# Two transformer-like blocks on one core: a seven-product matrix scheme rewritten without GpSimd, and four smaller moves of work

## The chip, the cores and the metric

One Trainium2 chip, one core. The metric is device time in microseconds (us) from one execution's start to its end; three runs of the kernel before gave 2943.02 to 2946.54, median 2946.03.

## The reference

512 tokens of width 1024, in float32, pass through one block of a first kind and two layers of a second kind.

```python
def first_block(x, ...):
    proj = rmsnorm(x, ln1_g) @ w_in               # q, k, v, pool, z, xbc, dt, gates
    y_a = dilated_attention_mixer(q, k, v, rel_bias) @ w_a
    y_b = pool_mixer(pool_in, pool_w, pool_scale) @ w_b
    y_c = ssd_mixer(z, xbc, dt_raw, ...) @ w_c    # state-space scan in chunks of 128
    x = x + (gates[0] * y_a + gates[1] * y_b + gates[2] * y_c) @ w_o
    x = x + conv_ffn(rmsnorm(x, ln2_g), ...)      # 2816 wide
    return rmsnorm(x, final_g)

def second_block(h, ...):                          # two layers
    proj = rms_norm(h, attn_norm[l]) @ w_in[l]
    a = differential attention; r = bidirectional retention; c = grouped-query attention
    h = h + (sum of gates[n] * (branch n @ w_branch[l, n])) @ w_out[l]
    h = h + square(relu(rms_norm(h, mlp_norm[l]) @ w_mlp_in[l])) @ w_mlp_out[l]   # 4096 wide
    return h
```

## The kernel before, in words

**Precision.** A float32 operand is split (`split`, L293) into a rounded high part, cast on ScalarE (L294), and a low part, subtracted on VectorE (L295). A product is then three matmuls: high by high, high by low, low by high. `feat` (L263) gives features by tokens, `tok` (L273) tokens by columns.

**Weights.** They come by SP's DMA queue into `raw` buffers of 128 x 1024 (`RAWS` of them, L25), and `halve` (L235) splits each into one `whi` and one `wlo` buffer (`HALVES` of each, L26). A block of 256 columns for all 1024 rows is two halves, a block of 512 columns is four (`wide`, L257).

**Pages.** Everything else lies in 47 pages of 128 x 512 (`Arena`, L50). PSUM has three `mm`, four `ax` and one `po` bank.

**Order.** The program is written in one order, with generators that are woven by step counts (`weave`, L178); a scheduler then fixes each engine's own order by when it expects operands to be ready, the program's order deciding between ready ones. At run time every engine works through its list in order.

**`quick` (L928)** multiplies a merged or hidden matrix of 512 tokens by a weight of at most 1024 rows and 1024 columns and adds the result to the residual pages X. It is Winograd's form of Strassen's scheme: both matrices are cut in 2 x 2 blocks, seven products in place of eight. It is called 14 times: for `w_o`, for three pieces of the feed-forward's second weight, and in each layer for `w_out` and four pieces of `w_mlp_out`. The token side is prepared by `Forms` (L68): each pair of finished pages r1, r2 (`add`, then `make`, L85) yields S1, S2, A11 - A21 and A12 - S2 by four operations on halves of pages, 128 x 256 (three on GpSimd, L89 to L91, one on VectorE, L92, which overwrites a half that L89 reads), and then the parts of all of them (`split`). The weight side takes four sums of weight blocks (`combine`, L948), each in two operations of 128 x 1024, of which the second is GpSimd's (L950). The seven products (`product`, L952) run in the order 1, 5, 3, 6, 2, 7, 4; products 1 and 5 leave out their last of four row blocks at first, since that is the pair of pages that gets ready last, and do it after both. Product 3 adds in PSUM to 5, and 4 to 7. Product 1, and later its sum with 6, is kept in two pages u, and `add_u` (L971, L973) adds these to X with eight GpSimd operations of 128 x 512. The other sums are `add` (L964) on VectorE.

**After some calls** come row norms. `rows` and `turn`, given to `quick`, make the norm of a row tile (`row_rstd`, L321, `norm_rows`, L333) and turn it by TensorE transposes into the next U (`norm_turn`, L341). `power` (L308) is GpSimd's x to the -1/2. At the end of the first block `rows` (L1127) does two norms at once, final and next, one power after the other.

**State-space scan** (`ssd`, L808): `start` (L838) multiplies a triangle of ones by high and low parts of the decays, 128 x 512 each, high on VectorE, low on GpSimd (L845).

**Grouped-query projection** (`gqa_proj`, L1520): keys and values, then queries, are projected, normed and rotated (GpSimd ends the rotation, L1227 and L1228), and `to_feat` turns them by transposes. In `layer` (L1637) it is chained between the rest of the first gate and three steps of the second (`take(gr, 3)`), woven with retention; grouped-query attention follows.

Of the kernel before, what the change touches and what calls it, by code (L numbers as in the profile page):

```python
# [10 lines left out]
F32 = mybir.dt.float32  # L11
F32R = mybir.dt.float32r
AF = mybir.ActivationFunctionType
# [11 lines left out]
RAWS = 5  # L25
HALVES = 6  # L26
# [44 lines left out]
class Forms:  # L71
# [13 lines left out]
    def make(self, r1, r2):  # L85
        B = self.body
        g, v, c, d = B.nc.gpsimd, B.nc.vector, slice(0, 256), slice(256, 512)
# [30 lines left out]
class Body:  # L118
# [189 lines left out]
    def power(self, out, x, n):  # L308
        self.nc.gpsimd.tensor_tensor(out, x, self.mhalf[:, :n], op=ALU.pow)

    def rstd(self, ss, n, eps):
        v, r = self.st(n), self.st(n)
        self.nc.vector.tensor_scalar(v, ss, eps, None, op0=ALU.add)
        self.power(r, v, n)
        return r
# [5 lines left out]
    def row_rstd(self, x, ss=None):  # L321

        nc = self.nc
        v, r = self.st(1), self.st(1)
# [315 lines left out]
    def gated(self, U, wg, g0, bias, y, wy, kt, acc, first, last, perm=False):  # L640
# [8 lines left out]
        for i in range(8 + AHEAD):  # L649
# [23 lines left out]
            t = T.pop(c)  # L673
            if first:
# [13 lines left out]
        self.free(y)  # L688
# [119 lines left out]
    def ssd(self, xs, BC, dt):  # L808
# [29 lines left out]
        def start(i):  # L838
# [4 lines left out]
            for q in range(2):  # L843
                for r, part, eng in zip(R[i][q], parts, (nc.vector, nc.gpsimd)):
                    eng.tensor_tensor(hl(r.t), self.tri.unsqueeze(1).to_broadcast([P, 4, P]),  # L845
                                      part[:, c, 8 * g + 4 * q:8 * g + 4 * q + 4].bitcast(F32).unsqueeze(2).to_broadcast([P, 4, P]), op=ALU.mult)
# [81 lines left out]
    def quick(self, w, k0, kt, F, X, scale=1.0, rows=None, turn=None):  # L928
# [8 lines left out]
        engines = (nc.vector, nc.gpsimd)  # L937
# [33 lines left out]
        def add_u(t, h, u):  # L971
            x = X[t][h].t
            nc.gpsimd.tensor_tensor(x, x, u.t, op=ALU.add)  # L973

# [15 lines left out]
        u = self.pgs(2)  # L990
# [15 lines left out]
        combine(b12, b22, b12, ALU.subtract)  # L1006
        b11 = [load(1, 1, j) for j in js]
        combine(b11, b12, b11, ALU.add)
        W6 = right(b11)
        for q in two:  # L1010
            add(q, 1, d[q])
        b = bank()
        product(6, W6, b)
        W7 = right(b12)
        b21 = [load(2, 1, j) for j in js]
        W2 = right(b21)
        for q in two:
            if scale == 1.0:
                nc.vector.tensor_tensor(u[q].t, u[q].t, b[q], op=ALU.add)
            else:  # L1020
                nc.vector.scalar_tensor_tensor(u[q].t, b[q], scale, u[q].t, op0=ALU.mult, op1=ALU.add)
            add_u(q, 1, u[q])
            sums(q)
        for q in two:
            add_u(2 + q, 1, u[q])
            add_u(2 + q, 0, u[q])
        e = bank()
        product(2, W2, e)
        combine(b21, b21, b11, ALU.subtract)
        for q in two:  # L1030
            add(q, 0, e[q])
# [746 lines left out]
```

## Time and profile before

| what | us |
|---|---|
| median of three runs | 2946.03 |
| the profiled execution | 2942.34 |
| its span, first to last instruction | 2940.2 |
| TensorE matmul busy | 2830.1 |
| VectorE busy | 2041.5 |
| ScalarE busy | 1307.2 |
| GpSimd busy | 938.3 |

The profile covers one execution. A matmul is listed from its start to a modelled end and overlaps the next, so a mean duration is longer than the distance between two starts. "Idle before" an instruction is put down to what released it last.

### The profile page before, as it was taken

What the parts mean: (1) busy time and instruction counts of PE and PEld (TensorE: products, weight loads), DVE (VectorE), ACT (ScalarE), POOL (GpSimd) and SP (SyncE); (2) the same over time, 40 slices, a digit from 0 to 9 for tenths busy, and PEclk for the clock granted to TensorE, in tenths of its full rate; (3) what the DMA queues carried; (4) which work ended last, traced back from release to release, by engine and by line L of the source; (5) the groups of instructions that cost most, each with busy time, mean ns of one, the idle gap of its engine ahead of it and who ended that gap; (6) DMA issues with size and microseconds to landing.
All of it is one profiled execution on the core that took longest, in us unless ns stands there. A gap on an engine that the chain in (4) does not pass through costs nothing.

```text
span 2940.2 us, 36920 instructions
## 1 busy us (share of the span) xinstructions
PE 2830.1 (96%) x13639; PEld 2361.2 (80%) x13639; DVE 2041.5 (69%) x3316; ACT 1307.2 (44%) x2249; POOL 938.3 (32%) x763
## 2 busy tenths in 40 slices
PE   8999999998999979999999899999999999989999
PEld 7888887887877868888787777787888887778777
DVE  4345477757778786856776787777765766877776
ACT  4344243334444445553464444444554455444443
POOL 0001105314132244211632344345321432534444
PEclk9999999999999989999999999999999999999999
DMA  7243331324242432222222332344222222323341
GB/s 217 82 126 105 100 97 55 88 77 151 74 142 72 133 112 87 88 75 73 73 69 68 118 112 88 101 130 149 84 65 89 64 67 61 122 83 115 115 129 65
DMA packets 225655, 288.20 MB, mean 98 GB/s; under 512 B 17769, under 2 KB 155331, under 8 KB 225475
## 3 DMA queue, kind: packets, MB, share of 16 engines
q1 hardware_dynamic: 212288, 272.77, 30.4%
q10 hardware_dynamic: 13187, 13.08, 1.5%
q8 instruction: 107, 1.75, 0.2%
q14 instruction: 73, 0.60, 0.1%
HBM read 276.30 MB, written 11.67 MB: 98 GB/s over the span
## 4 chain that ended last, share of the span: by engine, by line
PE 76%; DVE 8%; POOL 7%; DMA 4%; ACT 2%; issue 2%; ACTq 0%; SPq 0%; POOLq 0%; DVEq 0%
PE mm L270 14%; PE mm L269 14%; PE mm L271 14%; PE mm L280 4%; PE mm L281 4%; PE mm L282 4%; PE ax L960 4%; PE ax L961 4%; PE ax L962 4%; PE ax L301 3%; DVE wlo L295 3%; POOL raw L950 2%; DMA raw<-in_w_mlp_out_dram 2%; POOL pg L89 1%; DVE pg L295 1%
## 5 line engine op out<-in xcount | busy, mean ns | idle before, releaser
L295 DVE TENSOR_TENSOR wlo<-raw,whi 128x1024 fp32r<-128x1024 f32 (+3 forms) x554 | 730.3, 1325 | 276.6 <-ACT whi L294 269.1
L294 ACT CAST whi<-raw 128x1024 fp32r<-128x1024 f32 (+3 forms) x554 | 565.4, 1031 | 591.3 <-PE mm L270 318.0
L270 PE MATMUL mm<-ul,whi 128*128 128x512 f32 (+1 forms) x1792 | 689.2, 385 | 5.7 <-DVE ul L295 5.7
L269 PE MATMUL mm<-uh,whi 128*128 128x512 f32 (+1 forms) x1792 | 690.8, 387 | 2.0 <-ACT uh L294 2.0
L271 PE MATMUL mm<-uh,wlo 128*128 128x512 f32 (+1 forms) x1792 | 687.4, 384 | 0.0
L270 PEld LDWEIGHTS mm<-ul,whi 128*128 128x128 f32 x1792 | 340.7, 190 | 71.1 <-DVE ul L295 7.0
L269 PEld LDWEIGHTS mm<-uh,whi 128*128 128x128 f32 x1792 | 339.8, 190 | 66.8 <-ACT uh L294 2.9
L271 PEld LDWEIGHTS mm<-uh,wlo 128*128 128x128 f32 x1792 | 340.6, 190 | 64.7 <-issue 0.6
L960 PE MATMUL ax<-whi,pg 128*128 128x512 f32 x770 | 309.6, 406 | 55.2 <-ACT pg L294 43.8
L961 PE MATMUL ax<-wlo,pg 128*128 128x512 f32 x770 | 309.2, 402 | 0.0
L962 PE MATMUL ax<-whi,pg 128*128 128x512 f32 x770 | 298.0, 398 | 0.0
L280 PE MATMUL mm<-whi,uh 128*128 128x512 f32 (+3 forms) x736 | 280.5, 381 | 1.5 <-ACT uh L294 1.5
L281 PE MATMUL mm<-wlo,uh 128*128 128x512 f32 (+3 forms) x736 | 278.1, 378 | 0.0
L282 PE MATMUL mm<-whi,ul 128*128 128x512 f32 (+3 forms) x736 | 278.0, 378 | 0.0
L294 ACT CAST pg<-pg 128x512 fp32r<-128x512 f32 (+2 forms) x264 | 144.9, 574 | 261.8 <-DVE pg L92 66.3
L950 POOL TENSOR_TENSOR raw<-raw,raw 128x1024 f32<-128x1024 f32 (+1 forms) x56 | 159.2, 2843 | 314.7 <-DVE wlo L295 152.4
L973 POOL TENSOR_TENSOR pg<-pg,pg 128x512 f32<-128x512 f32 x112 | 209.6, 1895 | 91.0 <-ACT pg L998 48.5
L295 DVE TENSOR_TENSOR pg<-pg,pg 128x512 fp32r<-128x512 f32 (+2 forms) x264 | 198.1, 776 | 53.3 <-ACT pg L294 51.3
L960 PEld LDWEIGHTS ax<-whi,pg 128*128 128x128 f32 x770 | 149.3, 194 | 98.5 <-ACT pg L294 50.2
L89 POOL TENSOR_TENSOR pg<-pg,pg 128x256 f32<-128x256 f32 x55 | 59.1, 1075 | 421.5 <-DVE pg L1677 163.8
L301 PE MATMUL ax<-c_k_ident,pg 128*128 128x128 f32 x993 | 150.6, 279 | 33.4 <-DVE pg L1146 10.8
L962 PEld LDWEIGHTS ax<-whi,pg 128*128 128x128 f32 x770 | 149.4, 194 | 32.8 <-DVE pg L295 0.4
(264 smaller groups left out, 4387.1 us busy)
## 6 DMA issues: line engine op xcount, KB each, us to landing
raw<-in_w_in_dram SPq DMA_DIRECT2D x180, 512.0 KB, 3.7
raw<-in_w_mlp_out_dram SPq DMA_DIRECT2D x80, 512.0 KB, 3.6
raw<-in_w_mlp_in_dram SPq DMA_DIRECT2D x64, 512.0 KB, 4.3
raw<-in_ffn_w_up_dram SPq DMA_DIRECT2D x44, 512.0 KB, 3.8
raw<-in_ffn_w_down_dram SPq DMA_DIRECT2D x25, 512.0 KB, 3.5
raw<-in_w_out_dram SPq DMA_DIRECT2D x20, 512.0 KB, 3.7
raw<-in_w_branch_dram SPq DMA_DIRECT2D x16, 512.0 KB, 3.9
raw<-in_w_o_dram SPq DMA_DIRECT2D x10, 512.0 KB, 4.3
```

Source lines behind the costliest of these rows:

```text
L269: mm(ps, hi[:, cols], uh, start=k == 0, stop=False)
L270: mm(ps, hi[:, cols], ul, start=False, stop=False)
L271: mm(ps, lo[:, cols], uh, start=False, stop=k == nk - 1)
L280: mm(ps, uh, hi, start=k == 0, stop=False)
L281: mm(ps, uh, lo, start=False, stop=False)
L282: mm(ps, ul, hi, start=False, stop=k == n - 1)
L294: self.nc.scalar.copy(hi, src)
L295: self.nc.vector.tensor_tensor(lo, src, hi.bitcast(F32), op=ALU.subtract)
L301: self.nc.tensor.transpose(pt[:, i * P:(i + 1) * P], s, self.ident)
L960: mm(ps, uh[:, c], hi, start=not more and k == 0, stop=False, skip_group_check=more)
L961: mm(ps, uh[:, c], lo, start=False, stop=False, skip_group_check=more)
L962: mm(ps, ul[:, c], hi, start=False, stop=k == n - 1, skip_group_check=more)
```

## The change

`quick` is put in another order, 1, 2, 5, 6, 3, 7, 4, in which all of products 6, 7 and 4 add in PSUM to product 1, and product 2 has two `mm` banks of its own. The pages u and `add_u` are gone; all sums, those of weights and those of `Forms.make` too, are VectorE's. Each call loads as many weight blocks as before: the block B21 is read twice in place of B11. The other edits: 7 raw buffers and 5 half buffers; the low parts in `ssd.start` as four scaled ScalarE copies of 128 x 128 each; the gate steps in `gqa_proj` between the query projection and the turns; the two powers of `rows` from two means, r2 = (f + eps m + eps squared) to the -1/2, without the first power; and `free(y)` in `gated` at its last use.

```diff
-RAWS = 5
-HALVES = 6
+RAWS = 7
+HALVES = 5
...
-        g.tensor_tensor(s.t[:, c], r1.t[:, d], r2.t[:, d], op=ALU.add)
-        g.tensor_tensor(s.t[:, d], s.t[:, c], r1.t[:, c], op=ALU.subtract)
-        g.tensor_tensor(w.t[:, c], r2.t[:, c], s.t[:, d], op=ALU.subtract)
+        v.tensor_tensor(s.t[:, c], r1.t[:, d], r2.t[:, d], op=ALU.add)
         v.tensor_tensor(r1.t[:, d], r1.t[:, c], r1.t[:, d], op=ALU.subtract)
+        v.tensor_tensor(s.t[:, d], s.t[:, c], r1.t[:, c], op=ALU.subtract)
+        v.tensor_tensor(w.t[:, c], r2.t[:, c], s.t[:, d], op=ALU.subtract)
...
-        nc.vector.scalar_tensor_tensor(v, ss[:, 0:1], EPS, ss[:, 1:2], op0=ALU.add, op1=ALU.add)
-        self.power(r, v, 1)
-        return r
+        v = self.st(1)
+        nc.vector.tensor_tensor(v, ss[:, 0:1], ss[:, 1:2], op=ALU.add)
+        return self.rstd(v, 1, EPS)
...
+                hi, lo = [x[:, c, h0:h0 + 4].bitcast(F32) for x in parts]
+                for h in range(4):
+                    nc.scalar.activation(self.cols(R[i][q][1].t, h), self.tri, AF.Copy, scale=lo[:, h:h + 1])
...
         def combine(out, x, y, op):
-            for j, (o, a, b) in enumerate(zip(out, x, y)):
-                engines[j % 2].tensor_tensor(o, a, b, op=op)
+            for o, a, b in zip(out, x, y):
+                nc.vector.tensor_tensor(o, a, b, op=op)
...
         product(1, W1, a, b=n - 1)
-        u = self.pgs(2)
+        W2 = right([load(2, 1, j) for j in js])
+        e = [self.mm() for _ in two]
+        product(2, W2, e, b=n - 1)
+        product(1, W1, a, a=n - 1)
+        product(2, W2, e, a=n - 1)
         b12 = [load(1, 2, j) for j in js]
         combine(b11, b12, b11, ALU.subtract)
         W5 = right(b11)
         d = bank()
-        product(5, W5, d, b=n - 1)
-        product(1, W1, a, a=n - 1)
+        product(5, W5, d)
         for q in two:
-            nc.scalar.activation(u[q].t, a[q], AF.Copy, scale=scale)
-            add_u(q, 0, u[q])
-        product(5, W5, d, a=n - 1)
-        b22 = [load(2, 2, j) for j in js]
-        W3 = right(b22)
+            add(q, 0, a[q])
+        W6, W3 = [], []
+        for j in js:
+            t = load(2, 2, j)
+            combine([b11[j]], [t], [b11[j]], ALU.subtract)
+            W6 += right([b11[j]])
+            combine([b12[j]], [t], [b12[j]], ALU.subtract)
+            W3 += right([t])
+        for q in two:
+            add(q, 0, e[q])
+        product(6, W6, a, more=True)
         for q in two:
             add(2 + q, 1, d[q])
         product(3, W3, d, more=True)
+        for q in two:
+            add(q, 1, a[q])
+        W7 = right(b12)
         for q in two:
             add(q, 1, d[q])
             sums(q)
             if rows:
                 xn[q] = rows(q, ss[q])
-        c = bank()
-        product(7, W7, c)
+        product(7, W7, a, more=True)
+        b21 = [load(2, 1, j) for j in js]
+        combine(b21, b21, b11, ALU.subtract)
         W4 = right(b21)
         for q in two:
-            add(2 + q, 1, c[q])
+            add(2 + q, 1, a[q])
             sums(2 + q)
             if turn:
                 turn(q, xn[q])
-        product(4, W4, c, more=True)
+        product(4, W4, a, more=True)
         for q in two:
-            add(2 + q, 0, c[q])
+            add(2 + q, 0, a[q])
...
+                m, f = v[:, 0:1], v[:, 1:2]
+                nc.vector.tensor_tensor(m, ss[:, 0:1], ss[:, 1:2], op=ALU.add)
+                nc.vector.tensor_tensor(f, sf[:, 0:1], sf[:, 1:2], op=ALU.add)
+                nc.vector.scalar_tensor_tensor(f, m, EPS, f, op0=ALU.mult, op1=ALU.add)
+                r2 = self.rstd(f, 1, EPS * EPS)
+                r1 = self.rstd(m, 1, EPS)
...
         yield from self.proj_tok(l, U, 3584, 512, self.keep(xq, qthen))
+        yield from lead
         kT = yield from self.to_feat(yk, 2)
         qT = yield from self.to_feat(yq, 4)
...
-(self.chain(ga, self.gqa_proj(l, U), self.take(gr, 3)), 29))
+(self.chain(ga, self.gqa_proj(l, U, self.take(gr, 3))), 29))
```

## Rows read from the trace of the kernel before

**Rows 1.** Busy us of the engines; the core's mean granted clock.
```profile
PE 2830.1 (96%) x13639; PEld 2361.2 (80%) x13639; DVE 2041.5 (69%) x3316; ACT 1307.2 (44%) x2249; POOL 938.3 (32%) x763
...
core 0: 2940.2 us, clock 0.985
```
**Rows 2.** TensorE's waits, whole run: us in total, times, longest.
```profile
PE ax L960 <- ACT pg L294: 43.8, 14, 4.7
```
**Rows 3.** Busy time by stretch: features, then `quick`, of one MLP piece.
```profile
1847.00:1890.10 43.10, 43.10 (x191) 35.70 (x191) 29.30 (x34) 18.91 (x28) 14.31 (x11) 1.00 0.32 92
1890.10:1933.00 42.90, 40.75 (x171) 32.90 (x170) 32.23 (x33) 17.31 (x21) 23.09 (x13) 0.96 0.42 128
```
**Rows 4.** Timeline at that `quick`'s start (start, duration, idle before).
```profile
1892.95 0.68 DVE L1677 SCALAR_TENSOR_TENSOR pg<-mm,pg 128x512 f32<-128x512 f32 x1
...
1895.46 3.27 POOL L950 TENSOR_TENSOR raw<-raw,raw 128x1024 f32<-128x1024 f32 x1 [6.38 <-DMA raw<-in_w_mlp_out_dram]
1898.70 0.71 POOL L89 TENSOR_TENSOR pg<-pg,pg 128x256 f32<-128x256 f32 x1
...
1899.91 1.20 ACT L294 CAST pg<-pg 128x512 fp32r<-128x512 f32 x2 [4.67 <-DVE pg L92]
...
1900.58 0.50 PE L960 MATMUL ax<-whi,pg 128*128 128x512 f32 x1 [2.13 <-ACT pg L294]
```
**Rows 5.** Stretches: after that stop, later, after the next stop.
```profile
1900.58:1905.21 4.63, 4.61 (x13) 3.31 (x13) 3.63 (x5) 2.54 (x5) 0.69 (x1) 0.63 0.02 4
1906.00:1912.00 6.00, 6.00 (x28) 4.95 (x27) 5.50 (x5) 2.58 (x3) 3.10 (x4) 1.00 0.30 89
...
1987.00:1992.00 5.00, 4.92 (x20) 3.77 (x21) 4.84 (x7) 4.62 (x8) 2.62 (x3) 1.00 0.16 56
```
**Rows 6.** Groups (count, busy us, mean ns) and operations (min/median/max ns).
```profile
L973 POOL TENSOR_TENSOR pg<-pg,pg 128x512 f32<-128x512 f32 x112 | 209.6, 1895 | 91.0 <-ACT pg L998 48.5
L950 POOL TENSOR_TENSOR raw<-raw,raw 128x1024 f32<-128x1024 f32 (+1 forms) x56 | 159.2, 2843 | 314.7 <-DVE wlo L295 152.4
...
L92 DVE TENSOR_TENSOR pg<-pg x55: 410/426/965, 620.2 to 2903.2; 128x256 f32<-128x256 f32 x55
L950 DVE TENSOR_TENSOR raw<-raw,raw x56: 1210/1225/2201, 654.1 to 2916.8; 128x1024 f32<-128x1024 f32 x56
L967 DVE TENSOR_TENSOR pg<-pg,ax x110: 672/676/689, 826.6 to 2936.6; 128x512 f32<-128x512 f32 x110
...
L295 DVE TENSOR_TENSOR wlo<-raw,whi 128x1024 fp32r<-128x1024 f32 x521 | 702.3, 1355 | 246.2 <-ACT whi L294 238.7 <-PE ax L301 5.2
```
**Rows 7.** A `w_out` call: GpSimd's timeline, and TensorE's waits from 1600 to 1690.
```profile
1644.93 12.55 POOL L973 TENSOR_TENSOR pg<-pg,pg 128x512 f32<-128x512 f32 x6
...
PE ax L301 <- DVE pg L969: 2.3, 2, 1.2
```
**Rows 8.** The first block's last rows: VectorE's and TensorE's timeline.
```profile
1098.54 0.29 DVE L1293 TENSOR_TENSOR pg<-pg 128x128 f32<-128x128 f32 x1 [4.52 <-DMA pg<-in_diff_lam_k_dram]
...
1099.58 0.15 DVE L1143 TENSOR_TENSOR stats<-stats 128x1 f32<-128x1 f32 x1
...
1100.58 0.48 PE L301 MATMUL ax<-c_k_ident,pg 128*128 128x128 f32 x1 [10.79 <-DVE pg L1146]
```
**Rows 9.** The turns of q in the first layer: TensorE's timeline.
```profile
1433.88 0.48 PE L301 MATMUL ax<-c_k_ident,pg 128*128 128x128 f32 x1 [3.44 <-POOL pg L1228]
```
**Rows 10.** The scan's low parts (GpSimd); a scaled 128x128 copy (ScalarE).
```profile
L845 POOL TENSOR_TENSOR pg<-c_k_tri,ssd_a 128x512 fp32r<-128x512 f32 x16 | 22.4, 1412 | 125.6 <-DVE pg L773 114.9 <-PE ax L854 10.8
...
L1500 ACT ACTIVATE pg<-ax,ze 128x128 f32<-128x128 f32 x32 | 9.1, 368 | 4.7 <-PE ax L1491 3.2 <-POOL pg L1212 1.3
```
**Rows 11.** ScalarE's casts of weights that waited for TensorE.
```profile
ACT whi L294 <- PE mm L270: 318.0, 182, 7.3
```

More of the change, by code (lines that the diff above doesn't have):

```diff
@@ L305, in cols @@
         return x[:, c * P:(c + 1) * P]
-    def power(self, out, x, n):
-        self.nc.gpsimd.tensor_tensor(out, x, self.mhalf[:, :n], op=ALU.pow)
     def rstd(self, ss, n, eps):
@@ L313, in rstd @@
         self.nc.vector.tensor_scalar(v, ss, eps, None, op0=ALU.add)
-        self.power(r, v, n)
+        self.nc.gpsimd.tensor_tensor(r, v, self.mhalf[:, :n], op=ALU.pow)
         return r
@@ L323, in row_rstd @@
         nc = self.nc
-        v, r = self.st(1), self.st(1)
         if ss is None:
@@ L673, in gated @@
             t = T.pop(c)
+            if c == 7:
+                self.free(y)
             if first:
@@ L687, in gated @@
             yield
-        self.free(y)
         return forms
@@ L843, in start @@
             for q in range(2):
-                for r, part, eng in zip(R[i][q], parts, (nc.vector, nc.gpsimd)):
-                    eng.tensor_tensor(hl(r.t), self.tri.unsqueeze(1).to_broadcast([P, 4, P]),
-                                      part[:, c, 8 * g + 4 * q:8 * g + 4 * q + 4].bitcast(F32).unsqueeze(2).to_broadcast([P, 4, P]), op=ALU.mult)
+                h0 = 8 * g + 4 * q
+                hi, lo = [x[:, c, h0:h0 + 4].bitcast(F32) for x in parts]
+                nc.vector.tensor_tensor(hl(R[i][q][0].t), self.tri.unsqueeze(1).to_broadcast([P, 4, P]), hi.unsqueeze(2).to_broadcast([P, 4, P]), op=ALU.mult)
+                for h in range(4):
+                    nc.scalar.activation(self.cols(R[i][q][1].t, h), self.tri, AF.Copy, scale=lo[:, h:h + 1])
         def decays(i):
@@ L936, in quick @@
         parts = [(a, min(a + 2, n)) for a in range(0, n, 2)]
-        engines = (nc.vector, nc.gpsimd)
         def load(e, h, j):
@@ L1005, in quick @@
         product(3, W3, d, more=True)
[L1006 to L1009, printed above, removed]
+        for q in two:
+            add(q, 1, a[q])
+        W7 = right(b12)
         for q in two:
             add(q, 1, d[q])
[L1012 to L1022, printed above, removed]
-            sums(q)
[L1024 to L1031, printed above, removed]
+            sums(q)
             if rows:
                 xn[q] = rows(q, ss[q])
-        c = bank()
-        product(7, W7, c)
+        product(7, W7, a, more=True)
+        b21 = [load(2, 1, j) for j in js]
+        combine(b21, b21, b11, ALU.subtract)
         W4 = right(b21)
         for q in two:
-            add(2 + q, 1, c[q])
+            add(2 + q, 1, a[q])
             sums(2 + q)
@@ L1041, in quick @@
                 turn(q, xn[q])
-        product(4, W4, c, more=True)
+        product(4, W4, a, more=True)
         for q in two:
-            add(2 + q, 0, c[q])
+            add(2 + q, 0, a[q])
             if rows:
                 xn[2 + q] = rows(2 + q, ss[2 + q])
-        self.free(u, F)
+        self.free(F)
         return lambda: [turn(t, xn[t]) for t in (2, 3)] if turn else None
@@ L1127, in rows @@
             def rows(t, ss):
-                sf, v, r = self.st(2), self.st(2), self.st(2)
+                sf, v = self.st(2), self.st(3)
                 for h in (1, 0):
@@ L1135, in rows @@
                     self.square_sum(x, sf[:, h:h + 1])
-                nc.vector.scalar_tensor_tensor(v[:, 0:1], ss[:, 0:1], EPS, ss[:, 1:2], op0=ALU.add, op1=ALU.add)
-                self.power(r[:, 0:1], v[:, 0:1], 1)
-                r1, r2 = r[:, 0:1], r[:, 1:2]
-                nc.vector.tensor_tensor(v[:, 1:2], sf[:, 0:1], sf[:, 1:2], op=ALU.add)
-                nc.vector.tensor_scalar(v[:, 1:2], v[:, 1:2], r1, r1, op0=ALU.mult, op1=ALU.mult)
-                nc.vector.tensor_scalar(v[:, 1:2], v[:, 1:2], EPS, None, op0=ALU.add)
-                self.power(r2, v[:, 1:2], 1)
-                nc.vector.tensor_tensor(r2, r2, r1, op=ALU.mult)
+                m, f = v[:, 0:1], v[:, 1:2]
[4 more added lines that the diff above has]
+                r1 = self.rstd(m, 1, EPS)
                 xn = self.pgs(2, True)
@@ L1495, in across @@
             mv = self.st(8).rearrange("p (a b) -> p a b", b=2)
-            v, r = self.st(4), self.st(4)
             for qt in range(NT):
@@ L1503, in across @@
                 nc.vector.bn_aggr(mv[:, qt, :], bs[:, qt, :])
-            nc.vector.tensor_scalar(v, mv[:, :, 1], 1e-5, None, op0=ALU.add)
-            self.power(r, v, 4)
+            r = self.rstd(mv[:, :, 1], 4, 1e-5)
             for qt in range(NT):
@@ L1518, in ret_attn, with gqa_proj @@
         self.free(V, sr, dist, xk)
-    def gqa_proj(self, l, U):
+    def gqa_proj(self, l, U, lead):
         nc, I = self.nc, self.I
@@ L1645, in layer @@
         _, (r, _) = self.weave((self.diff_attn(*d, aT), 36), (self.chain(self.ret_proj(l, U), self.take(ga, 3)), 28))
-        _, (_, g, _) = self.weave((self.ret_attn(*r, rT), 19), (self.chain(ga, self.gqa_proj(l, U), self.take(gr, 3)), 29))
+        _, (_, g) = self.weave((self.ret_attn(*r, rT), 19), (self.chain(ga, self.gqa_proj(l, U, self.take(gr, 3))), 29))
         self.weave((self.gqa_attn(*g, cT), 53), (self.chain(gr, self.take(gc, 3)), 16))
```

5 lines of the change are left out of this document (1 added, 4 removed).

## The prediction

> **What bounds the kernel now.** I read the busy shares first. TensorE is busy 2830.1 of 2940.2 us, VectorE 2041.5, GpSimd 938.3 [rows 1]. No edit here removes a matmul (seven block products per `quick` call before and after), so the most that can be won is the 110 us in which TensorE stands still, and what its clock loses around these stops: a granted clock of 0.985 over 2940.2 us is 45 us of full-speed time not granted [rows 1].
>
> The second view is what TensorE waited for [rows 2]. One entry holds 43.8 us of the 110: 14 waits of an accumulating matmul (L960) for a ScalarE cast of a page. Fourteen is the number of `quick` calls, so it is one wait per call, 3.1 us each. The next largest, 10.79 us, happens once [rows 8].
>
> The third view is two adjoining stretches of the second block's MLP, 43.1 us of features and 42.9 us of `quick` [rows 3]. In the features TensorE is full and starts a matmul every 43.1/191 = 0.226 us; in `quick` it lacks 2.2 us, VectorE is busy 32.2 of 42.9 and GpSimd 23.1. The fourth is the start of that `quick`, engine by engine [rows 4]. The reader is to follow a chain backwards. TensorE resumes at 1900.58 after 2.13 us, released by the cast that began at 1899.91. That cast waited for the VectorE subtraction in `Forms.make` (L92), which overwrites what GpSimd reads in L89; GpSimd began L89 only at 1898.70. Yet the input of L89 was there when the VectorE product that began at 1892.95 and took 0.68 us ended, at 1893.63. Between stands L950, a sum of weights that no product needs for another ten microseconds: it came first in GpSimd's queue, waited 6.38 us for its load and ran 3.27. So the wait is not GpSimd's load but its order and its speed.
>
> The stop costs more than its length. In the 4.63 us after it the granted clock is 0.63, a mix of 2.4 and 1.2 GHz; later it is 1.00 again [rows 5]. 4.63 x 0.37 = 1.7 us are lost. After the next call's stop the clock stays at 1.00 [rows 5], so not every stop pays it: I take 19 us over the fourteen, four fifths of 14 x 1.7 = 24.
>
> **The change, part by part.**
>
> *`quick` and `Forms.make` leave GpSimd.* Gone from GpSimd are 112 page sums (209.6 us), 56 weight sums (159.2 us) [rows 6] and 165 half-page operations; gone from ScalarE 28 copies. VectorE gets 56 x 1.225 = 69 us of weight sums, 165 x 0.426 = 70 us of half pages, and 2 more page sums per call (14 for 12), 28 x 0.676 = 19 us: together 158 us. But VectorE's own operations are now stretched while GpSimd runs: the 1024-wide low parts take 1.355 us in the mean, where a weight sum of the same size takes 1.21 at best, 1.225 in the median and 2.20 at worst [rows 6]. 521 x 0.13 us alone is 68 us; with most two-input GpSimd work gone I take half of the added time back. Over the kernel VectorE then stands near 2120 us, well under TensorE.
>
> In one `quick` it is tighter. 32.2 us [rows 3], plus four weight sums (4.9), two page sums (1.35), three half-page operations (1.3), less some 3 us of stretching, is 36.7 us. TensorE's 168 matmuls need 168 x 0.226 = 37.9 us. VectorE fits, at 97%.
>
> The chain at the start becomes: product ends, two VectorE half pages (0.85), a cast (0.6, half of the two in [rows 4]), a subtraction (0.7), some 2.2 us after 1893.63, so 1896, while the 36 matmuls that cover it last to 1898.4, where the stop began. The first stretch keeps its 36 matmuls, now from two products whose weights are bare loads (A11 B11 and A12 B21), so no weight sum has to precede them. So the 43.8 us and the 19 us of clock can go, 62.8 in all. I don't take all: VectorE is in order and 97% full, and the sum that waits for a load can stand before `make` there too. I put back 1.0 us per call and the clock loss of a third of them (14.0 + 6.3): **-42**. Bounds: -63 when nothing is put back, and the far end is the slower rival below.
>
> *`quick` with norms behind it.* In a `w_out` call six GpSimd sums hold 12.55 us, behind them the row norm and the turns; TensorE then lost 2.3 us to late turns [rows 7]. Three calls are of this kind. The sums go; VectorE, with the norm's products and the last weight sum in a product's 24 matmuls, 5.4 us, is what comes late next, and the turns of the first two row tiles wait for it. **-4**, between -7 (three times this wait) and +6 (1 us more on each of two turns in three calls).
>
> *Norm powers.* The last feed-forward rows get one power and three tiny operations of 0.15 us less in a row [rows 8], and the two powers no longer follow each other. TensorE's 10.79 us there end with L1146, but 4.52 us of them VectorE stood at L1293, a product that waits for lambda's loads and came first in its queue [rows 8]. This is a matter of order that the edit needn't touch. **-3**, between 0 and -10.8. `row_rstd` gains one such operation in 20 rows; most lie beside products: **+1**, between 0 and 3.0.
>
> *Gate steps ahead of the turns.* TensorE waited 3.44 us for the rotation before the turns of q [rows 9]; the other layer has a like wait. Three gate features (72 matmuls, 16 us) now lie in that hole: 2 x 3.44 = 6.9 us, and 2 x 1.7 if the clock falls each time as it did above. The same 16 us no longer cover the way from the turned q and k to the first scores: a copy, two casts and two subtractions, about 3 us a layer, though retention's last steps and later gate steps may cover it. Bounds -10.3 and +6; **-7**.
>
> *State-space low parts.* 16 GpSimd operations of 1.41 us become 64 ScalarE copies; the nearest row, a scaled 128x128 copy, takes 0.368 [rows 10]: 23.6 us on an engine that is idle for most of that stage, and 22.4 us off the GpSimd chain. **-1**, between -4 and +4.
>
> *Seven raw buffers, five half buffers.* More raw buffers can only bring loads forward. Half buffers are the currency of the whole kernel: ScalarE waits 318.0 us, 182 times, until TensorE gives one back [rows 11]. One less takes a quarter product (6 x 0.226 = 1.36 us) off the lead. A block of four halves keeps about 3 us of lead after a cast and a subtraction (2.3 us). Between 0 and 18 such blocks x 1.36 = 25 us; I take **+2**, since the casts wait for TensorE and not the other way round. `free(y)` two steps earlier costs and brings nothing: the arena has pages.
>
> Sum: -42 - 4 - 3 + 1 - 7 - 1 + 2 = **-54**. The profiled execution took 2942.3 us (span 2940.2), which gives 2888; the median of the runs, 2946.0, is 3.7 above it: **2892 us**.
>
> **Rivals.** (a) *All waits go.* VectorE keeps up and `make` comes early: -63 - 7 - 10.8 - 10.3 - 4, about -95, so 2851. For it: every one of the waits has a GpSimd operation or a queue's order behind it. Against: 97% in `quick`.
>
> (b) *The wait changes its queue.* A weight sum waiting for its load stands before `make` on VectorE as it did on GpSimd. Then half of the start waits remain: 31 us back, about 2920. For it: the order that put L950 first is still made by readiness. Against: seven raw buffers hold all that the first three products need.
>
> (c) *Slower: VectorE becomes the bound of `quick`.* Now it idles 10.7 us of each 42.9. With 36.7 us of work, a call gets longer than now as soon as VectorE still idles more than 6.2 us in it, for loads, for casts and for half buffers that TensorE gives back late. With 8 us it is 1.8 us per call, +25, less 11 from the other edits: 2960. For it: queues in order and one half buffer less. Against: TensorE is what VectorE's casts wait for today, so the idle time is mostly lead. The Trainium skill (Trace Analysis, Identifying the Most-Contended Engine) says to relieve the engine with the highest occupancy; by that rule a change that gives work to the second busiest is a step towards this rival, and moving it off the least busy wins nothing by itself. The trace bears this out only in part: VectorE is at 75% of the `quick` stretch [rows 3], and it is the least busy of the three that TensorE waits for at its start [rows 4].
>
> (d) *It doesn't take hold:* the start wait stays and the moved work hides: the total within 6 us of 2946. That is (c) at its point of balance.
>
> **How the numbers follow.** The forecast (2870 to 2915) has 0.48; (a) 0.14; (b) 0.17, of which all is faster by more than 0.2%; (d) 0.06; (c) 0.15. About 0.2% (6 us) is what a measurement of this kernel tells from no change. Faster 0.79, same 0.06, slower 0.15. The range 2860 to 2950 leaves out part of (a) and most of (c), some 2 in 10.
>
> **What would show it.** Right: the entry L960 after a page cast falls from 43.8 us to under 15; GpSimd's busy time falls below 450 us; the half-speed stretches after `quick` starts thin out; VectorE's 1024-wide low parts come near 1.23 us; the two rotation waits vanish. Wrong: `quick` stretches of 43 us with VectorE at 40 busy, or TensorE waiting there for page sums (L964's adds) or weight casts, which would be (c); a weight sum released by a load just ahead of `make` on VectorE, which would be (b); new waits for casts in the projections, which would be the half buffers.

## The result, and the profile after

The median fell from 2944.53 us (four runs, 2940.38 to 2946.54) to **2858.62 us** (four runs, 2856.82 to 2859.05). The ratio is 0.9709, with a 95% interval of 0.9692 to 0.9726. The profiled execution of the new kernel took 2858.8 us. The forecast was 2892 with a range of 2860 to 2950: the direction was right, but the forecast gain of 54 us falls short of the real 86 by over a third, and the median lies 1.4 us below the range. The rival in which all waits go (2851) came nearest.

Busy times and clock, from the first part of the page and the view of the core, as in [rows 1]:

```profile
span 2857.0 us, 36632 instructions
PE 2803.2 (98%) x13639; PEld 2344.4 (82%) x13639; DVE 2012.7 (70%) x3585; ACT 1316.8 (46%) x2285; POOL 386.9 (14%) x414
core 0: 2857.0 us, clock 0.996
```

TensorE stood still for 2857.0 - 2803.2 = 53.8 us, where it had been 110.1: that is 56 of the 83 us that the span lost. The other 27 are TensorE's own busy time, the same 13639 matmuls in 2803.2 instead of 2830.1 us, with the granted clock up from 0.985 to 0.996. GpSimd lost 551 us. VectorE got 269 instructions more and is busy 28.8 us *less*. Added up one by one, its instructions last 2214.0 us before and 2214.3 after; busy time is smaller because neighbours overlap in the list and an overlap counts once.

What TensorE waited for, whole run (total, times, longest):

```profile
PE ax L301 <- DVE pg L335: 10.1, 2, 9.4
PE ax L301 <- POOL pg L1212: 9.6, 4, 3.8
PE ax L301 <- DVE pg L1130: 5.4, 1, 5.4
PE ax L959 <- DVE pg L966: 4.2, 4, 1.3
...
PE ax L959 <- DVE pg L968: 2.7, 2, 1.3
```

The largest is the start-up. The wait of the accumulating matmul for a page cast (43.8 us, 14 times [rows 2]) is down to one of 1.4 us. The same MLP piece as in [rows 3], each call cut here from its first product matmul to its last, before and then after (PE, PEld, DVE, ACT, POOL busy, clock, DMA share, GB/s):

```profile
1849.77:1890.12 40.35, 40.35 (x179) 33.43 (x178) 28.64 (x33) 18.00 (x28) 14.31 (x11) 1.00 0.28 80
1890.12:1935.72 45.60, 43.45 (x183) 35.16 (x182) 32.90 (x34) 18.22 (x22) 23.09 (x13) 0.96 0.44 137
```

```profile
1806.87:1847.22 40.35, 40.35 (x179) 33.41 (x178) 31.26 (x45) 18.84 (x28) 0.00 (x0) 1.00 0.25 78
1847.22:1888.47 41.25, 41.25 (x183) 34.16 (x182) 31.69 (x39) 17.11 (x19) 0.00 (x0) 1.00 0.49 154
```

The features are unchanged to the hundredth. The call went from 45.60 to 41.25 us, with TensorE full and the clock at 1.00. VectorE's load in it fell, with the work of GpSimd added.

The new start of that call, engine by engine (start, duration), stands against [rows 4]:

```profile
1847.22 0.39 PE L959 MATMUL ax<-whi,pg 128*128 128x512 f32 x1
...
1849.48 0.68 DVE L1660 SCALAR_TENSOR_TENSOR pg<-mm,pg 128x512 f32<-128x512 f32 x1
...
1850.08 1.21 DVE L949 TENSOR_TENSOR raw<-raw,raw 128x1024 f32<-128x1024 f32 x1
...
1851.21 0.42 DVE L89 TENSOR_TENSOR pg<-pg,pg 128x256 f32<-128x256 f32 x1
...
1852.15 1.22 DVE L949 TENSOR_TENSOR raw<-raw,raw 128x1024 f32<-128x1024 f32 x1
...
1853.73 1.15 ACT L294 CAST pg<-pg 128x512 fp32r<-128x512 f32 x2 [1.85 <-DVE pg L90]
...
1855.09 0.42 DVE L92 TENSOR_TENSOR pg<-pg,pg 128x256 f32<-128x256 f32 x1
```

A weight sum (L949) still stands ahead of `make` (L89), and a second one between its steps, but each holds the queue for 1.2 us and none waits for its load. From the end of the product (1850.16) to the end of the casts (1854.88) it is 4.7 us; before, from 1893.63 to 1901.11, it was 7.5. The 36 matmuls in front last 36 x 0.226 = 8.1 us, to 1855.4, and the casts are there at 1854.9, half a microsecond before the stop would have begun.

VectorE's operations on two inputs, against [rows 6] (busy us, mean ns, then idle):

```profile
L295 DVE TENSOR_TENSOR wlo<-raw,whi 128x1024 fp32r<-128x1024 f32 x521 | 642.8, 1239 | 288.3 <-ACT whi L294 287.1 <-DMA c_k_rope_axi<-in_k_rope_axi_dram 0.3
L949 DVE TENSOR_TENSOR raw<-raw,raw 128x1024 f32<-128x1024 f32 x108 | 131.3, 1218 | 5.4 <-DMA raw<-in_w_out_dram 1.9 <-DMA raw<-in_w_o_dram 1.8 <-DMA raw<-in_w_mlp_out_dram 0.8
L295 DVE TENSOR_TENSOR pg<-pg,pg 128x512 fp32r<-128x512 f32 x193 | 129.2, 685 | 3.4 <-ACT pg L294 3.2
```

The 521 weight low parts went from 1355 to 1239 ns, the 193 page low parts from 854 to 685. By stage, with a call counted from the start of its first product matmul to that of its last, the span lost:

| stage | before to after, us |
|---|---|
| `quick` for w_o (block 1) | 44.87 to 38.81 |
| three FFN calls | -1.09, -1.33, -6.72 |
| MLP calls, layer 0 | -6.46, -4.42, -4.35, -5.97 |
| MLP calls, layer 1 | -5.82, -4.80, -3.25, -4.41 |
| two `w_out` calls | -6.29, -6.33 |
| **fourteen calls together** | **-67.3** |
| all ahead of w_o, state space among it | -1.35 |
| features behind w_o and the two `w_out` | -1.88, -3.37, -5.31 |
| attention of layer 0 and lambda; of layer 1 | -3.92; +0.01 |
| **between the calls together** | **-15.8** |

### The profile page after: what moved, and what is told of

Same layout as the page of the kernel before. It is cut to its first block, busy times and chain, and to the rows that moved or that the text cites. A ratio compares the mean times of both kernels' runs of the same rounds, so it can differ in the third digit from the quotient of the medians.

```text
span 2857.0 us, 36632 instructions
## 1 busy us (share of the span) xinstructions
PE 2803.2 (98%) x13639; PEld 2344.4 (82%) x13639; DVE 2012.7 (70%) x3585; ACT 1316.8 (46%) x2285; POOL 386.9 (14%) x414
## 4 chain that ended last, share of the span: by engine, by line
PE 85%; DVE 8%; POOL 3%; DMA 2%; issue 1%; ACT 1%; ACTq 0%; SPq 0%; POOLq 0%; DVEq 0%
PE mm L270 16%; PE mm L269 16%; PE mm L271 16%; PE ax L959 4%; PE ax L961 4%; PE ax L960 4%; PE mm L280 4%; PE mm L282 4%; PE mm L281 4%; PE ax L301 3%; DVE wlo L295 2%; POOL stats L312 1%; PE po L1343 1%; PE ax L1247 1%; PE ax L1248 1%
## 5 line engine op out<-in xcount | busy, mean ns | idle before, releaser
L295 DVE TENSOR_TENSOR wlo<-raw,whi 128x1024 fp32r<-128x1024 f32 (+3 forms) x554 | 668.9, 1214 | 314.5 <-ACT whi L294 309.5
L959 PE MATMUL ax<-whi,pg 128*128 128x512 f32 x660 | 253.6, 392 | 8.2 <-DVE pg L966 4.2
L960 PE MATMUL ax<-wlo,pg 128*128 128x512 f32 x660 | 255.7, 390 | 0.0
L961 PE MATMUL ax<-whi,pg 128*128 128x512 f32 x660 | 252.9, 392 | 1.0 <-DVE pg L295 1.0
L312 POOL TENSOR_TENSOR stats<-stats,mhalf 128x1 f32<-128x1 f32 (+3 forms) x84 | 91.0, 1087 | 1193.5 <-DVE stats L327 612.8
L301 PE MATMUL ax<-c_k_ident,pg 128*128 128x128 f32 x993 | 151.6, 279 | 25.4 <-DVE pg L335 10.1
L295 DVE TENSOR_TENSOR pg<-pg,pg 128x512 fp32r<-128x512 f32 (+2 forms) x264 | 160.3, 629 | 6.2 <-ACT pg L294 5.8
L301 PEld LDWEIGHTS ax<-c_k_ident,pg 128*128 128x128 f32 x993 | 123.5, 144 | 49.1 <-POOL pg L1212 11.0
L282 PEld LDWEIGHTS mm<-whi,ul 128*128 128x128 f32 x736 | 139.3, 189 | 25.6 <-DVE ul L295 3.1
L280 PEld LDWEIGHTS mm<-whi,uh 128*128 128x128 f32 x736 | 139.7, 190 | 24.6 <-ACT uh L294 1.2
L281 PEld LDWEIGHTS mm<-wlo,uh 128*128 128x128 f32 x736 | 139.7, 190 | 23.1 <-DVE wlo L295 0.6
```

The costliest lines, as they stand in the source:

```text
L280: mm(ps, uh, hi, start=k == 0, stop=False)
L281: mm(ps, uh, lo, start=False, stop=False)
L282: mm(ps, ul, hi, start=False, stop=k == n - 1)
L295: self.nc.vector.tensor_tensor(lo, src, hi.bitcast(F32), op=ALU.subtract)
L301: self.nc.tensor.transpose(pt[:, i * P:(i + 1) * P], s, self.ident)
L959: mm(ps, uh[:, c], hi, start=not more and k == 0, stop=False, skip_group_check=more)
```

## The experiments

Each kernel stands beside the kernel before in its own series (medians 2943.84, 2946.61 and 2943.13); where two are compared I use medians, or the ratio times 2944.5.

**1. Which move of work matters, with the new order?** From the new kernel, either `make`'s three operations or every second weight sum goes back to GpSimd.

```diff
-        v.tensor_tensor(s.t[:, c], r1.t[:, d], r2.t[:, d], op=ALU.add)
+        g.tensor_tensor(s.t[:, c], r1.t[:, d], r2.t[:, d], op=ALU.add)
...
```

> The changed kernel with the three half-page operations of Forms.make back on GpSimd, all else as changed. Queue theory (the start wait of quick came from a weight sum that stood before make in GpSimd's queue): GpSimd now holds little but powers, make starts at once, its chain is some 1 us longer but has 2 us of cover; 2851 to 2868 us, fewer than 6 us of waits for page casts at quick starts. Speed theory (GpSimd's make itself is too slow, and it stretches VectorE): 2880 us or more, with waits of 1 us or more at most of the 14 starts.

```diff
-                nc.vector.tensor_tensor(o, a, b, op=op)
+                (nc.vector, nc.gpsimd)[(j + j0) % 2].tensor_tensor(o, a, b, op=op)
```

> The changed kernel with every second weight sum of quick on GpSimd again, make staying on VectorE. Queue theory: make no longer stands behind a weight sum, so the start waits stay away; what is left is VectorE being stretched and sums that take 2.5 us for 1.2; 2858 to 2875 us. Speed theory: the sums come too late for their casts and TensorE waits in each call; 2890 us or more. VectorE's busy time should rise by about 40 us of stretching although it does 52 operations less.

Measured: 2862.84 us (0.9695 to 0.9747) and 2864.29 us (0.9705 to 0.9754), 4 and 6 us above the new kernel and as the queue theory has it. In both, the MLP calls stay within 0.15 us of the new kernel's. With `make` on GpSimd the two `w_out` calls get 1.6 us longer each, with the sums there 5.5 and 5.1, and TensorE's waits in the second kernel (total, times, longest) name what they wait for, a page sum late on VectorE:

```profile
PE ax L959 <- DVE pg L968: 11.5, 2, 5.7
```

So GpSimd's slowness in `make` alone costs little once no weight sum stands ahead of it in that queue. And 56 operations less on VectorE relieve it of nothing: it is busy 2029.8 us, 17 more than in the new kernel, its low parts at 1327 ns (groups of that kernel's VectorE):

```profile
L295 DVE TENSOR_TENSOR wlo<-raw,whi 128x1024 fp32r<-128x1024 f32 x521 | 688.3, 1327 | 286.3 <-ACT whi L294 284.9
```

**2. The same moves with the old order.** To the kernel before: `make` on VectorE, the weight sums on VectorE, both; and both with the page sums (L973) as well, so that nothing of `quick` is left on GpSimd. Their edits are those above, turned round, and for the last

```diff
-            nc.gpsimd.tensor_tensor(x, x, u.t, op=ALU.add)
+            nc.vector.tensor_tensor(x, x, u.t, op=ALU.add)
```

> The kernel before with Forms.make alone moved to VectorE. Queue theory (make stood behind a weight sum in GpSimd's queue): this frees it, so the 14 start waits (43.8 us) and their clock loss go whatever the product order is: 2880 to 2895 us. Order theory (it takes the new product order, whose first two products need no weight sums): the wait stays in most calls, 2925 us or more.

> The kernel before with all weight sums on VectorE and make on GpSimd. Queue theory: GpSimd's queue still holds the eight page sums but nothing that waits for a load, so make starts at once, as well as in the run above: 2880 to 2900 us. Rival (the sum that waits for its load now stands in front of make's one operation and of the splits on VectorE): the wait stays, 2925 us or more.

> The kernel before with make and weight sums on VectorE; the product order and the page sums of u on GpSimd stay. Queue theory: within 6 us of the better of the two runs above, since either alone frees make. What then still separates it from the changed kernel (2858) is the page sums on GpSimd behind the norms and the new order; 2875 to 2895 us.

> The kernel before with make, all weight sums and the page sums of u on VectorE: no GpSimd in quick, but the old product order with its eight page sums. GpSimd theory (its slow page sums behind the norms and its stretching of VectorE make the rest): most of the 45 us between the run with make and sums moved (2903) and the changed kernel go, 2862 to 2880 us. Order theory (product 5's weight sums and VectorE's 37 us of work hold TensorE): 2890 us or more.

Measured: 2903.30 (0.9835 to 0.9872), 2910.27 (0.9858 to 0.9911), 2903.04 (0.9834 to 0.9875) and 2894.32 (0.9824 to 0.9853). The first three lie above what the queue theory said, and the fourth is where the order theory had it. Either move alone frees `make` from the queue, and both together give no more than one. The wait at the start falls from 43.8 us to between 16.9 and 20.0 and stays there, even in the last kernel, where GpSimd has no part in it. TensorE's waits in the third kernel, then in the fourth, where the wait of the last feed-forward rows has grown too:

```profile
PE ax L960 <- ACT pg L294: 17.6, 7, 5.3
```

```profile
PE ax L960 <- ACT pg L294: 16.9, 7, 4.8
PE ax L301 <- DVE pg L1146: 14.4, 1, 14.4
```

The seven waits that stay in these two kernels are in the three FFN calls, the two `w_out` calls and the first MLP call of each layer. The new kernel with the old buffers (experiment 5) has 0.3 us of this entry left, so it is the new order that removes them. In the old order the second product needs a weight sum and its cast. The fourth kernel's first `w_out` call shows both ahead of the page casts (VectorE, ScalarE, TensorE):

```profile
1620.29 0.42 DVE L89 TENSOR_TENSOR pg<-pg,pg 128x256 f32<-128x256 f32 x1
1621.23 1.22 DVE L950 TENSOR_TENSOR raw<-raw,raw 128x1024 f32<-128x1024 f32 x1 [0.52 <-DMA raw<-in_w_out_dram]
...
1622.53 1.04 ACT L294 CAST whi<-raw 128x1024 fp32r<-128x1024 f32 x1 [2.92 <-DVE raw L950]
1623.48 1.13 ACT L294 CAST pg<-pg 128x512 fp32r<-128x512 f32 x2
...
1624.15 0.80 PE L960 MATMUL ax<-whi,pg 128*128 128x512 f32 x1 [3.69 <-ACT pg L294]
```

The sum and its load hold VectorE for 1.7 us between two steps of `make`, so they explain a part of this stop of 3.7; the other calls were not followed back in this way. Leaving GpSimd gives 48 us of the 86; the rest needs the new order of products and the other edits.

**3. Order without the two moves.** The new kernel with both edits of experiment 1; the new product order and the end of `u` and its page sums remain, with the small edits.

> The changed kernel with make and every second weight sum on GpSimd again: of the rewrite of quick only the product order and the end of the page sums u remain. Queue theory: sums stand before make in one queue again, the start waits return: 2890 to 2915 us. Order theory: the new order alone removes them, 2862 to 2875 us, what the two single undoings cost together (4 + 6 us).

Measured: 2879.91 us (0.9749 to 0.9793), between what the two theories said. Order and small edits alone are worth 67 us, the two moves alone 43, all 86: they overlap by 24. Call by call, some 26 us of the start wait are removed by either, so that is probably the overlap. An MLP call of this kernel (columns as in the stretches above) shows what VectorE's busy share is worth as a measure:

```profile
1865.19:1906.54 41.35, 41.35 (x183) 34.10 (x182) 35.25 (x36) 16.98 (x19) 9.36 (x5) 1.00 0.49 153
```

VectorE carries 35.25 us, near the 36.7 that I had feared, and the call takes 41.35, where the new kernel's takes 41.25: nothing is lost. What this kernel loses, it loses mostly in the w_o, FFN and `w_out` calls (1.0 to 4.4 us each) and in the first MLP call of each layer (1.5).

**4. The load that the prediction assumed.** To the new kernel, a useless 128x512 subtraction or addition on VectorE behind each of the eight weight sums of a call; its result is thrown away.

```diff
                 nc.vector.tensor_tensor(o, a, b, op=op)
+                with self.tmp() as junk:
+                    nc.vector.tensor_tensor(junk, o[:, :512], b[:, :512], op=op)
```

> The changed kernel with one useless 128x512 VectorE operation behind each of the eight weight sums of a quick call, 5.4 us per call: VectorE's work in an MLP quick stretch rises from 31.5 to the 37 us that the prediction assumed. Load theory (the prediction had the load too high, but its margin right): waits of about 1 us per call and some clock loss appear, 2872 to 2890 us. Margin theory (VectorE's lead of 2.5 products carries 37 us in 41 without a wait): 2856 to 2866 us.

Measured: 2885.75 us (0.9790 to 0.9823), 27 us back, as the load theory has it. The calls get 32.5 us longer in all: the eight MLP calls 0.4 to 1.8 each, 1.2 in the mean, the two `w_out` calls 6.5 and 6.9. The third MLP call of layer 0, then TensorE's waits over the whole run:

```profile
1861.78:1904.45 42.67, 41.59 (x184) 34.09 (x183) 35.23 (x45) 16.89 (x19) 0.00 (x0) 1.00 0.46 149
```

```profile
PE ax L963 <- DVE pg L295: 11.1, 6, 2.2
...
PE ax L961 <- ACT pg L294: 8.1, 5, 1.8
...
PE ax L961 <- DVE pg L968: 5.8, 6, 1.8
```

VectorE is at 35.23 us here, short of the 37 that I wanted and the same as in experiment 3, yet this call is 1.4 us longer and TensorE waits 1.1 of them. So the busy time alone doesn't set the cost. That it is the place in the queue that does, right behind the weight sums and ahead of `make` and the low parts, is an argument and not shown: in experiment 3 `make` and half of the sums run on GpSimd, and VectorE has 36 instructions in the call, not 45. The mechanism of the slower rival exists, near the size that I had put back for it (20 us); the change simply doesn't reach the load that sets it off in the MLP calls.

**5. The small edits, one by one.** The gate steps go back behind the turns; the buffers back to five and six; the last rows' norm back to its two powers in a row.

```diff
-        yield from lead
...
-RAWS = 7
-HALVES = 5
+RAWS = 5
+HALVES = 6
...
-                m, f = v[:, 0:1], v[:, 1:2]
...
+                nc.vector.tensor_scalar(v[:, 1:2], v[:, 1:2], r1, r1, op0=ALU.mult, op1=ALU.mult)
...
```

> The changed kernel with the three gate steps behind the turns again in program order. Theory: the scheduler had put the gate matmuls among the turns before the change too, and the wait for the last rotation (3.3 and 3.8 us) is the length of the norm and rotation chain of the last query tile; so no difference, 2855 to 2863 us, and waits of 3 to 4 us per layer at the turns in either order. Rival (the prediction): the edit is worth 7 us, so 2866 us.

> The changed kernel with 5 raw and 6 half buffers as before. Theory: with 5 raw buffers the sums of quick wait for loads on VectorE, in front of make: waits for page casts come back in part, 2865 to 2890 us. Rival (buffers don't matter, the half buffer given up costs what the raw ones bring): 2853 to 2864 us.

> The changed kernel with rows() as before, one power after the other. Theory of the powers: the shorter chain lets the norm's products come ahead of lambda's product in VectorE's list, so the 10.8 us wait returns, 2863 to 2870 us. Rival (the order changed for other reasons, the removed GpSimd page sums): 2857 to 2862 us.

Measured: 2857.50 (0.9677 to 0.9735), 2867.20 (0.9716 to 0.9769) and 2860.34 us (0.9702 to 0.9731). The lead does nothing. The old buffers cost 8.6 us: their fastest run (2865.51) is slower than the slowest of the new kernel. In the MLP the features get 1.59 us shorter and the call 1.59 longer, so nothing remains there; 3.0 and 4.4 us come in the features behind the two `w_out` calls, 2.0 behind w_o and 3.0 in the attention of layer 1, and the wait of the last feed-forward rows doubles (TensorE's waits with the old buffers):

```profile
PE ax L301 <- DVE pg L1130: 10.9, 1, 10.9
```

The time is in the range of the theory but its cause is not: the idle time before VectorE's weight sums, most of it for loads, does rise from 5.4 to 25.9 us, yet TensorE's waits for page casts did not come back. What grew is waits around the row norms. Whether the raw or the half buffers bring the 8.6 us was not tried apart.

The old powers bring the wait of the last rows back to 9.3 us, but the run is only 1.7 us slower, within the scatter. The order on VectorE is what the theory of the powers said. In the new kernel the norm's products (L1130) go ahead of lambda's product, which waits for its load; with the old powers lambda's (L1278 there) stands in front again, as before the change (VectorE's timeline, new kernel, then old powers):

```profile
1075.97 2.74 DVE L1130 SCALAR_TENSOR_TENSOR pg<-pg,stats,pg 128x512 f32<-128x512 f32 x4 [0.39 <-POOL stats L312]
1081.61 0.29 DVE L1277 TENSOR_TENSOR pg<-pg 128x128 f32<-128x128 f32 x1 [2.90 <-DMA pg<-in_diff_lam_k_dram]
```

```profile
1080.72 0.29 DVE L1278 TENSOR_TENSOR pg<-pg 128x128 f32<-128x128 f32 x1 [2.92 <-DMA pg<-in_diff_lam_k_dram]
1080.93 2.73 DVE L1131 SCALAR_TENSOR_TENSOR pg<-pg,stats,pg 128x512 f32<-128x512 f32 x4
```

**6. The waits that remain.** In the new kernel the gain of grouped-query q and the last step of the rotation of q and k go from GpSimd to VectorE, and lambda's block goes behind the two projections (that move is left out below).

```diff
-            xv = self.head_norm(xq[t].t, 8, gq)
+            xv = self.head_norm(xq[t].t, 8, gq, nc.vector)
...
-            nc.gpsimd.tensor_tensor(o1, a, b, op=ALU.subtract)
-            nc.gpsimd.tensor_tensor(o2, c, d, op=ALU.add)
+            (eng or nc.gpsimd).tensor_tensor(o1, a, b, op=ALU.subtract)
+            (eng or nc.gpsimd).tensor_tensor(o2, c, d, op=ALU.add)
...
```

> The changed kernel with diff_proj's lambda block moved behind the two projections, and the gain and the last step of the rotation of grouped-query heads on VectorE. Order theory: the wait of 5.4 us and the 1.4 us behind it at the first block's end shrink by some 3 us, most of what is left being the norm chain itself; the two turn waits (3.3 and 3.8 us) fall under 1 us each, since the rotation no longer queues behind powers on GpSimd, with 3.4 us of clock: 2844 to 2854 us. Rival (VectorE is too full there, the chain only changes engines): 2856 to 2866 us.

Measured: **2850.31 us** (2847.19 to 2854.70; ratio 0.9673 to 0.9701), 8 us under the new kernel by the medians and the best of all: its slowest run lies below the new kernel's fastest. The two attention stages are 5.39 and 5.71 us shorter. TensorE's waits in it:

```profile
PE ax L301 <- DVE pg L1130: 5.5, 1, 5.5
...
PE ax L301 <- POOL pg L1212: 2.6, 2, 1.3
```

The two long waits of the rotation are gone; the two of 1.3 us that stay stand where the new kernel has them too, early in each attention stage. The 5.5 us of the last feed-forward rows stand as they were: in the new kernel lambda's product already stood behind the norm's, so moving it could win nothing there, and I was wrong that this wait still hangs on it. What is left is probably the norm's own chain through GpSimd's power, with a weight's low part and another product in its way on VectorE (last section); no run shortened it.

## Why the prediction was right or wrong

**Where the wait comes from: right.** A weight sum waiting for its load ahead of `make` on GpSimd was put down as the cause. Taking away either of the two from that queue (experiment 2) takes 24 to 27 of the 43.8 us, the new order takes the rest, and putting `make` back without the sums (experiment 1) brings no wait. The prediction named both, the queue and the two products whose weights are bare loads. Its chain at the start was too short: 2.2 us were reckoned, and it is 4.7 to the end of the casts, since two weight sums stand in it. The 36 matmuls covered that with 0.5 us to spare. The signs named beforehand came: the entry fell to 1.4 us (under 15 was asked), GpSimd to 386.9 us (under 450), the low parts to 1239 ns (near 1230), the clock to 0.996.

**What failed first: the put-back in `quick`.** The step was VectorE's load of one call, 36.7 us or 97%, and from it "I put back 1.0 us per call and the clock loss of a third of them". Measured: 31.69 us in a call of 41.25, 77%. A part of the 97% was the measure: 36.7 was set against the 37.9 us of the 168 product matmuls, but the call's stretch also holds 15 matmuls of the next features and lasts 41.25 us, of which 36.7 would be 89%. The load itself was too high too. From 32.90 in the exact call, with 7.55 added, 8.8 us are missing. 2.9 of these lie ahead in the features (a weight sum, a weight's low part and a half page's). Some 4.4 are stretching that went, where I took 3. The rest is mostly overlap: an operation adds less busy time than its listed duration. The call's low parts, before and after (count, busy us, mean ns, then idle):

```profile
L295 DVE TENSOR_TENSOR wlo<-raw,whi 128x1024 fp32r<-128x1024 f32 x14 | 20.0, 1440 | 4.2 <-ACT whi L294 4.1
```

```profile
L295 DVE TENSOR_TENSOR wlo<-raw,whi 128x1024 fp32r<-128x1024 f32 x13 | 15.8, 1219 | 4.1 <-ACT whi L294 4.1
```

Over the kernel it is alike: compared shape by shape, the operations that both kernels have on VectorE got 156 us shorter in all, as much as the 158 that were added, where I had credited half. So nothing had to be put back in the MLP calls, and -42 was the mis-sized term: the fourteen calls gave -67.3, which holds the `w_out` norms too and which the -63 without a put-back fits.

**The share alone doesn't tell the cost.** In the new kernel's first `w_out` call VectorE is busy 42.06 of 43.47 us, the very 97%, and TensorE waits 1.3 us in it, for a page sum (L968). That is near the 1.0 us that I put back, so the danger was real. That stretch:

```profile
1587.96:1631.43 43.47, 42.13 (x188) 34.21 (x187) 42.06 (x60) 23.61 (x36) 1.10 (x2) 1.00 0.60 188
```

But experiments 3 and 4 have 35.2 us in an MLP call, once free and once for 1.4 us. What stands ahead of the operation that TensorE needs next is the likely reason. With extra load put there the MLP calls grow by 1.2 us in the mean, so the price of the danger was fair and the load was not. That the whole kernel then takes 2885.75, near the forecast, is chance in part, since other terms were wrong as well.

**Rival (c), the slower one, and the rule beside it.** The Trainium skill (Perfetto Trace Analysis, Identifying the Most-Contended Engine) wants the engine with the highest occupancy relieved first. The record doesn't speak against that: by busy share the busiest is TensorE (matmuls 96%, weight loads 80%), and its waits are what the change took away. What failed is the step that the prediction took from the rule. This change gave instructions to the second busiest and took them from the idlest, and won 86 us; the busy share of VectorE before contained time that GpSimd caused. (At the call's start VectorE was not the least busy of the three, as the prediction read it: from 1893.63 to 1900.58 ScalarE has 2.24 us, VectorE 2.36 and GpSimd 4.96.) One sign of (c) came in a small measure: TensorE waits for page sums (L966, L968) six times, 6.9 us in all, none of it in an MLP call.

**`w_out` with norms behind it (-4): too small.** Its calls lost 6.3 us each, like the others, and the features behind them 3.37 and 5.31 more, in part because the turns no longer come late: the L301 <- L969 wait of [rows 7] has no counterpart after.

**Buffers (+2): wrong sign.** The size was between 0 and 18 blocks of 1.36 us, for half buffers alone; I gave the two more raw buffers nothing. Together they are worth 8.6 us, and it comes behind w_o and `w_out` and in the attention of layer 1 (experiment 5). It is still the casts that wait for TensorE, now even longer than in [rows 11] (ScalarE's waits after):

```profile
ACT whi L294 <- PE mm L270: 353.6, 195, 7.7
```

**Gate steps ahead of the turns (-7): zero.** The reading of [rows 9] was right that TensorE waits for the rotation, wrong that nothing filled the hole. The scheduler had already put gate matmuls among the turns before; now they come in one piece ahead of them and the wait is still there (TensorE's timeline after):

```profile
1422.38 1.69 PE L301 MATMUL ax<-c_k_ident,pg 128*128 128x128 f32 x14
...
1427.54 0.69 PE L301 MATMUL ax<-c_k_ident,pg 128*128 128x128 f32 x2 [3.25 <-POOL pg L1212]
```

Its length is that of the last q tile's chain on GpSimd, whose power, gain and rotation run one behind the other (GpSimd's timeline after):

```profile
1419.77 1.65 POOL L312 TENSOR_TENSOR stats<-stats,mhalf 128x8 f32<-128x8 f32 x1
1422.29 2.13 POOL L1196 TENSOR_TENSOR pg<-pg,hg 128x512 f32<-128x512 f32 x1 [0.87 <-DVE pg L1195]
...
1427.04 0.45 POOL L1212 TENSOR_TENSOR pg<-pg 128x128 f32<-128x128 f32 x1 [0.23 <-DMA raw<-in_w_in_dram]
```

Without the lead the entry is the same (10.0 us, 4 times); experiment 6 took that chain to VectorE and the wait went. Of the good signs named beforehand this one failed: "the two rotation waits vanish".

**Powers (-3): the size may fit, the reason doesn't. Row norm (+1), state space (-1): not told apart.** The last rows' wait went from 10.79 to 5.4 us, of which experiment 5 gives 3.9 to the edit, though the run lost only 1.7, within the scatter. I had called lambda's place a matter of order that the edit needn't touch, but the edit changes it, and so do others: the wait is 10.9 again with the old buffers and in experiment 3, whose powers are the new ones. All stages ahead of w_o together gave -1.35, but with the old powers, which share all code of these stages, they take 3.05 us longer, so this says nothing of the state-space term. The row norm was not measured by itself.

## What to carry to other kernels

Where VectorE and GpSimd both do operations on two inputs, moving work from GpSimd to VectorE can leave VectorE no busier; don't price it by adding durations to the busy time. In an in-order queue look for the operation that can wait for a load and is needed late: here a sum that waited 6.38 us for its load held up an operation of 0.7 us that TensorE needed [rows 4]. Start an accumulation with the products whose operands need no preparation, and before moving work into a hole, see whether the schedule on the chip has filled it already.

## What the hardware showed that I had not expected

The size of the stretching. A 128x1024 low part on VectorE takes 1239 ns with GpSimd nearly out of `quick`, 1245 in the old order with nothing of `quick` on GpSimd, 1355 in the kernel before with 938 us of GpSimd work, and 1387 where only `make` was moved (772 us). It isn't proportional to GpSimd's busy time: what runs there beside the low parts matters. The two kernels of experiment 1 have 566 and 567 us of GpSimd work. With the weight sums there the low parts take 1327 ns; with `make` there they take 1247, and it is the one operation of `make` left on VectorE (L92 there) that goes from 420 to 830. By the second of these kernels, 56 weight sums there (180 us of GpSimd) saved VectorE 56 x 1.22 = 68 us and left it 17 us busier, so they stretched its other work by some 85 us, about half their own length.

The stretching goes the other way too. Of GpSimd's 36 one-column powers after the change, 30 take 0.54 to 0.57 us, one of them after a rest of 321 us. The other six take 1.0 to 2.1 us. Each of the six starts while VectorE is in an operation that reads two SBUF tiles (L295 on a weight, L335, L1119) and ends 0.4 us behind it, or behind a second one that follows at once. Five of the 30 start inside a VectorE operation too, but in each of these one input is in PSUM. The longest stands in the norm of the last feed-forward rows, ahead of the products (L1130) with which TensorE's wait of 5.4 us ends. It takes 1.6 us more than most, and VectorE, which is to do those products next, is busy with the same two operations until 1075.5. So up to 1.6 us of that wait lie in what stands there on VectorE; no run moved it (VectorE's and GpSimd's timeline after):

```profile
1073.71 1.21 DVE L295 TENSOR_TENSOR wlo<-raw,whi 128x1024 fp32r<-128x1024 f32 x1
1073.80 2.14 POOL L312 TENSOR_TENSOR stats<-stats,mhalf 128x1 f32<-128x1 f32 x1 [2.20 <-DVE stats L311]
1074.84 0.68 DVE L1119 TENSOR_TENSOR pg<-pg,pg 128x512 f32<-128x512 f32 x1
```
